# Reordering the opening stage of a transformer step: the order in which tokens, modulation weights and first products are taken

## The chip, the cores and the metric

The kernel runs on one core of a Trainium2 chip. The metric is the device time of one execution, in microseconds (us). The engines are TensorE (PE; its weight loads are PEld), VectorE (DVE), ScalarE (ACT), GpSimd (POOL) and SyncE (SP, which here only issues DMAs). Each engine works through its own list of instructions in the order in which the program wrote them, and waits where an operand of the next one isn't there yet.

## The reference, cut to what matters

One layer of a diffusion backbone runs over 1152 tokens (1024 latent ones, 128 context ones) of width 1024, in float32. The part that the change touches is the way from the tokens to the first columns of the input projection:

```python
mod = (silu(cond) @ w_mod + b_mod)[:, None, :]
sh1, sc1, g1, sh2, sc2, g2 = split(mod, 6)
h = rmsnorm(x, g_pre_mix) * (1.0 + sc1) + sh1
proj = h @ w_in        # q, k, v, xr, gr, xf
```

Behind it stand attention, a linear recurrence, a Fourier mixing, the output projection and a SwiGLU network, which are the other 95% of the time.

## The kernel before

Tokens lie in nine tiles of 128, three to a **chunk** of 384 columns (n = 0, 1, 2; the third chunk holds 256 latent and 128 context tokens). The width of 1024 is cut into eight slices (k = 0 to 7). Every product in full float32 precision is three matmuls in the fp32r type (mm3, L184 to L186): high part of the weights by low part of the data, high by high, low by high. So each operand is first split into a high part (a copy into fp32r) and a low part (the operand less its high part).

The opening stage makes h, transposed, and the first two of fourteen **units** (128 columns each) of the input projection. Its order is a table of short words, START, that a loop walks through; each word records its instructions at the end of the lists of their engines. Numbers behind a letter are its arguments:

- X t: load tile t of the tokens (SP). Q t: its squares summed on ACT, then the root of the mean on POOL (L178, L180). N t: the tile is scaled by it on DVE (L303).
- T n k0 k1 u m: PE turns slices k0 to k1 - 1 of chunk n (L313), in both tables always one slice, which is three transposes, into the bank psu[u][m]. C n k0 k1 e: the bank is copied to SBUF (xT), on DVE with e = 0, on ACT with e = 1.
- M s q: load a quarter of the modulation weights of step s (512 KB, six buffers). A s: 64 small matmuls that make shift and scale of slices 2s and 2s+1 (L345), and a copy (rows). B s: one transpose (L353) and four small DVE operations that leave them in M and S1 (L358, L359).
- L i: load the weights of unit i (two buffers). W i: their high part, on ACT. V i: their low part, on DVE.
- m n k: shift and scale of chunk n, slice k, twice: on ACT straight into the high part hh (L330), on DVE into u (L331). r n k e: the low part hl = u less hh, on DVE with e = 0, on POOL with e = 1 (L174).
- s n k: PE adds slice k of chunk n to units 0 and 1, six matmuls of 384 columns. The sums stand in psu[0][n] and psu[1][n], two of the same six banks that the transposes use, for all eight slices. One such word is called a **step** below; there are 24.
- D: PE multiplies zeros, before the first tokens are there. E: a small load that is used after the stage.

SP issues the loads in the order of X, M, L and E; a load into a buffer that is still read waits, and all loads behind it. Four large buffers hold the three chunks of tokens and then, in turn, the turned chunks xT. When the table is done, the six banks are copied out and the loop over units 2 to 13 (from L804 on) keeps PE at work.

Of the kernel before, what the change touches and what calls it, by code (L numbers as in the profile page):

```python
# [9 lines left out]
F32 = mybir.dt.float32  # L10
# [6 lines left out]
P = 128  # L17
D = 1024
# [6 lines left out]
NCH = T // CW  # L25
# [110 lines left out]


START = """
D9 D7 X0 Q0 X1 Q1 X2 X3 N0 X4 N1 Q2 X5 Q3 N2 Q4 T07802 X6 N4 T04510 T05611 T06712 X7 L0 C0781
C0451 C0561 C0671 Q5 T03402 T00110 T01211 T02312 N3 Q6 C0340 Q7 X8 C0010 C0120 C0230 N5 T11200  # L140
T12301 M00 N7 C1121 C1231 N6 T15611 T16712 T10110 T13400 T14501 Q8 C1341 C1451 W0 C1560 C1670
T17812 N8 M01 M02 M03 T25601 T26702 V0 C1011 T20110 T21211 A0 C2011 C2121 L1 M10 C2561 C2671
T23401 W1 C1780 M11 B0 M12 m10 r101 V1 C2341 T24502 T27812 m11 T22300 C2451 m00 C2231 r110 s10
C2781 r000 m21 M13 m20 r200 s11 m01 r010 M20 s00 A1 s20 M21 r210 B1 m02 M22 s01 M23 m03 r021 m22
s21 m23 M30 M31 r221 A2 r230 M32 m12 s02 m13 r120 L2 r130 s22 s23 M33 E B2 m14 s12 m05 r031 m04 r050
r141 r041 s13 s03 m24 L3 A3 m25 r250 s14 m15 B3 r150 m16 r241 r160 m26 s04 s24 m06 r061 m17 W2
r261 r170 m27 s05 m07 W3 s25 r271 V2 s15 s16 r071 s17 s06 V3 s26 L4 s07 L5 s27
"""

_OUTS = {"y": (T, D), "new_k": (P, 512), "new_v": (P, 512), "new_h": (2, 256)}  # L150
# [2 lines left out]
def _body(tc, nc, A):  # L153
    PE, ACT, DVE, POOL, SP = nc.tensor, nc.scalar, nc.vector, nc.gpsimd, nc.sync

    def pool(name, bufs=1, side="left", space=None, **kw):
        if space is not None:
            kw["space"] = space
        return tc.alloc_tile_pool(name=name, bufs=bufs, side=side, **kw)
# [34 lines left out]
    X1 = tc.dram_tile([T, D], F32, name="X1")  # L194
# [21 lines left out]
    st = pool("startup")  # L216
# [565 lines left out]
    f = P_["kq"] = pool("kq")  # L782
# [829 lines left out]
    for v, (g, cs) in enumerate(VIS):  # L1612
        last = v == NV_ - 1
        for c_ in ([(c,) for c in cs] if last else [cs]):
# [6 lines left out]
            for p in range(7):  # L1621
# [131 lines left out]
```

## Time and profile before

| | us |
|---|---|
| median of three runs | 1435.22 (1434.53, 1435.22, 1440.06) |
| the profiled execution | 1430.3, with a span of 1428.5 |
| PE busy | 1375.9 (96% of the span) |
| DVE, ACT, POOL busy | 822.0, 573.4, 427.6 |

The span is the time from the first to the last instruction in the trace; 1.8 us of the profiled execution lie around it. All times of rows below are from the start of the span. A busy PE is not a PE at its peak, since the ends of matmuls are modelled.

### The profile page before, as it was taken

To read this page: it belongs to the slowest core of one execution; us is meant where nothing else is said; L and a number is where in the kernel's file an instruction comes from. 1 tells how busy PE (TensorE), PEld (TensorE's weight loads), DVE (VectorE), ACT (ScalarE), POOL (GpSimd) and SP (SyncE) were. 2 spreads that over 40 slices of the span, in tenths; PEclk is the share of its full clock that TensorE was granted. 3 is DMA by queue.
4 is the path that set the end of the run, shared out by engine and by line. 5 is a ranking of instruction groups with operands and counts; after the bars stand their busy time and mean duration, and the time that the engine had idled before them with its cause. 6 is when DMAs were issued, how large, how long until landed. Compare 5 with 4: busy or idle time off the path is not lost.

```text
span 1428.5 us, 22758 instructions
## 1 busy us (share of the span) xinstructions
PE 1375.9 (96%) x8918; PEld 1248.9 (87%) x8918; DVE 822.0 (58%) x1247; ACT 573.4 (40%) x1138; POOL 427.6 (30%) x426
## 2 busy tenths in 40 slices
PE   7899999998999999998999999999999989999998
PEld 6887799888889888887899999999999968888886
DVE  5724464564888843667866767667666653243232
ACT  6511136734888863555322323223222342142120
POOL 2301111222666662447634334333423100000000
PEclk9999999999999999999999999999999999999999
DMA  8558840147755335563222312222222472334541
GB/s 328 178 202 276 266 158 31 63 158 174 179 136 146 96 108 166 176 209 111 78 93 64 101 59 93 84 74 99 67 77 82 137 275 89 115 109 166 182 151 59
DMA packets 108326, 193.40 MB, mean 135 GB/s; under 512 B 7701, under 2 KB 77754, under 8 KB 104762
## 3 DMA queue, kind: packets, MB, share of 16 engines
q1 hardware_dynamic: 108074, 191.41, 41.7%
q8 instruction: 71, 1.16, 0.4%
q10 hardware_dynamic: 144, 0.52, 0.1%
q14 instruction: 37, 0.30, 0.1%
HBM read 146.67 MB, written 45.24 MB: 134 GB/s over the span
## 4 chain that ended last, share of the span: by engine, by line
PE 49%; DVE 2%; issue 1%; ACT 1%; DMA 1%; POOL 0%; DVEq 0%; POOLq 0%; SPq 0%; ACTq 0%
PE g L186 10%; PE g L184 10%; PE g L185 10%; PE d L186 6%; PE d L184 6%; PE d L185 6%; DVE gu L174 1%; DMA hr<-HB 1%; DVE av L174 0%; ACT gu L168 0%; DMA raw_gu<-in_w_down 0%; DVE u L1530 0%; DVE hf L1530 0%; DVE hd L174 0%; ACT av L168 0%
## 5 line engine op out<-in xcount | busy, mean ns | idle before, releaser
L186 PE MATMUL g<-av,gu 128*128 128x320 f32 (+1 forms) x1232 | 364.2, 296 | 7.7 <-DVE gu L174 7.3
L184 PE MATMUL g<-av,gu 128*128 128x320 f32 (+1 forms) x1232 | 364.3, 296 | 1.2 <-ACT av L168 0.8
L185 PE MATMUL g<-av,gu 128*128 128x320 f32 (+1 forms) x1232 | 363.1, 295 | 0.0
L186 PEld LDWEIGHTS g<-av,gu 128*128 128x128 f32 x1232 | 232.1, 188 | 10.3 <-DVE gu L174 10.2
L184 PEld LDWEIGHTS g<-av,gu 128*128 128x128 f32 x1232 | 231.9, 188 | 2.3 <-issue 1.4
L185 PEld LDWEIGHTS g<-av,gu 128*128 128x128 f32 x1232 | 232.2, 188 | 0.0
L174 DVE TENSOR_TENSOR gu<-raw_gu,gu 128x512 fp32r<-128x512 f32 x139 | 141.2, 1023 | 40.1 <-ACT gu L168 40.1
L184 PE MATMUL pu<-hl,w 128*128 128x384 f32 x336 | 123.0, 366 | 4.6 <-POOL hl L174 3.8
L186 PE MATMUL pu<-hh,w 128*128 128x384 f32 x336 | 113.1, 337 | 0.0
L185 PE MATMUL pu<-hh,w 128*128 128x384 f32 x336 | 113.1, 337 | 0.0
L184 PE MATMUL d<-dw,hd 128*128 128x512 f32 x270 | 106.7, 395 | 3.2 <-DVE dw L174 3.1
L186 PE MATMUL d<-dw,hd 128*128 128x512 f32 x270 | 106.4, 394 | 0.9 <-DVE hd L174 0.9
L185 PE MATMUL d<-dw,hd 128*128 128x512 f32 x270 | 106.4, 394 | 0.0
L1371 POOL TENSOR_TENSOR raw_gu<-raw_gu,t 128x512 f32<-128x512 f32 x25 | 33.2, 1329 | 233.4 <-DVE gu L174 233.4
L1530 DVE TENSOR_TENSOR u<-g,u 128x320 f32<-128x320 f32 (+1 forms) x176 | 77.5, 450 | 29.8 <-PE g L186 29.8
L940 PE MATMUL s<-ks,qs 128*128 128x384 f32 x384 | 91.0, 358 | 3.0 <-ACT p L953 1.5
L946 DVE TENSOR_REDUCE nm<-s 128x1 f32<-128x1152 f32 x64 | 86.6, 1353 | 9.4 <-PE s L940 9.2
L953 ACT ACTIVATE p<-s,nm 128x1152 f32<-128x1152 f32 x64 | 78.2, 1222 | 29.5 <-DVE nm L946 16.4
L1672 ACT ACTIVATE t<-d 128x512 f32<-128x512 f32 x18 | 10.7, 596 | 186.4 <-PE d L186 186.4
L168 ACT ACTIVATE gu<-raw_gu 128x512 fp32r<-128x512 f32 x139 | 83.4, 620 | 3.5 <-DMA raw_gu<-in_w_down 3.4
L1080 POOL TENSOR_SCALAR fv<-fv 128x1 f32<-128x1 f32 x9 | 2.7, 303 | 271.5 <-ACT t L1672 271.5
L184 PEld LDWEIGHTS pu<-hl,w 128*128 128x128 f32 x336 | 63.3, 189 | 21.7 <-issue 14.1
(276 smaller groups left out, 2867.4 us busy)
## 6 DMA issues: line engine op xcount, KB each, us to landing
raw_gu<-in_w_gu SPq DMA_DIRECT2D x25, 1024.0 KB, 4.8
hr<-HB SPq DMA_DIRECT2D x32, 704.0 KB, 5.0
wmb<-in_w_mod SPq DMA_DIRECT2D x32, 512.0 KB, 5.0
raw_gu<-in_w_down SPq DMA_DIRECT2D x22, 512.0 KB, 4.2
HB<-hf SPq DMA_DIRECT2D x18, 576.0 KB, 3.1
x<-in_x SPq DMA_DIRECT2D x18, 512.0 KB, 4.6
wm<-in_w_mod SPq DMA_DIRECT2D x16, 512.0 KB, 7.7
raw<-in_w_in_u SPq DMA_DIRECT2D x14, 512.0 KB, 7.7
```

The source lines that it names most:

```text
L168: ACT.activation(out, in_, AF.Copy)
L174: eng.tensor_tensor(out, x, hi.bitcast(F32), op=OP.subtract)
L184: PE.matmul(out, wh, xl, start=first, stop=False)
L185: PE.matmul(out, wh, xh, start=False, stop=False)
L186: PE.matmul(out, wl, xh, start=False, stop=last)
L940: PE.matmul(b[:, j, :CW], q[:, st_, m, i * P:(i + 1) * P], ks[:, m, j * CW:(j + 1) * CW], start=(st_ == 0), stop=(st_ == 1))
L946: DVE.tensor_reduce(nm, s, axis=AX.XY, op=OP.max, negate=True)
L953: ACT.activation(p.rearrange("p (n c) -> p n c", c=CW), s, AF.Exp, bias=nm, accum_out=ss)
L1080: POOL.tensor_scalar(v[:, 0:1], v[:, 0:1], v[:, 1:2], D * EPS, op0=OP.add, op1=OP.add)
L1371: POOL.tensor_tensor(b21, b21, t2, op=OP.subtract)
L1530: add = lambda out, x: DVE.tensor_tensor(out, b, x, op=OP.add)
L1672: ACT.activation(t2, b, AF.Square, accum_out=fv[:, t, n:n + 1])
```

## The change

The table START is replaced, and nothing else of weight is: the three token buffers are now named before the loop and not at the first load of each chunk (they come in the same order as before). The words are the same ones but for three things: every low part r has e = 0, so none is left on POOL (eleven of 24 were there); of the 24 copies C, twelve are on DVE (seven were), and T takes the banks in another order; the order of the words is new throughout. As all lines behind the table move down by one, L184 to L186 are L185 to L187 in the changed kernel, L174 is L175 and so on.

```diff
 START = """
-D9 D7 X0 Q0 X1 Q1 X2 X3 N0 X4 N1 Q2 X5 Q3 N2 Q4 T07802 X6 N4 T04510 T05611 T06712 X7 L0 C0781
...
+D9 D7 X0 Q0 X1 Q1 X2 Q2 M00 M01 M02 M03 N0 N1 N2 X3 X4 X5 L0 L1 X6 X7 X8
...
-    raws, wsl, xts, xch, xT = {}, {}, {}, {}, {}
+    raws, wsl, xts, xT = {}, {}, {}, {}
+    xch = [st.tile([P, 3, D], F32, name=f"x{n}", tag="x", bufs=4) for n in range(NCH)]
 
     def load_x(t):
         n, i = divmod(t, 3)
-        if i == 0:
-            xch[n] = st.tile([P, 3, D], F32, name=f"x{n}", tag="x", bufs=4)
```

On SP the loads stood as nine token tiles, with unit 0's weights ahead of the ninth, then the sixteen quarters of modulation weights, with unit 1's weights behind the first four. Now they stand as three token tiles, four quarters, three token tiles, the weights of units 0 and 1, three token tiles, and twelve quarters; units 2 and 3 come behind all of these.

Three places show what that does to the lists. In the names, x0, x1, x2 are the chunks of tokens, xT0 to xT2 the same turned, pu with two digits is the bank psu[u][m], mod and rows belong to A, modt to B, w0 and w1 are the split weights of units 0 and 1, and ssx holds the sums of squares.

ScalarE, from the first squares on, in the kernel before:

```order
L299 ACTIVATE hh_88,ssx_115<-x0_142 128x1024 x3
L299 ACTIVATE hh_88,ssx_115<-x1_152 128x1024 x2
L168 ACTIVATE xT0_186<-pu02_119 128x384
L168 ACTIVATE xT0_186<-pu10_120 128x384
L168 ACTIVATE xT0_186<-pu11_121 128x384
L168 ACTIVATE xT0_186<-pu12_122 128x384
L299 ACTIVATE hh_88,ssx_115<-x1_152 128x1024
L299 ACTIVATE hh_88,ssx_115<-x2_171 128x1024 x2
L168 ACTIVATE xT1_228<-pu00_117 128x384
L168 ACTIVATE xT1_228<-pu01_118 128x384
L299 ACTIVATE hh_88,ssx_115<-x2_171 128x1024
```

and in the changed one, from the squares of chunk 1 on:

```order
L299 ACTIVATE hh_88,ssx_118<-x1_109 128x1024 x3
L330 ACTIVATE hh_88<-xT0_196,M_80,S1_81 128x384 x2
L169 ACTIVATE w0_280<-raw0_171 128x1024
L169 ACTIVATE w1_283<-raw1_173 128x1024
L169 ACTIVATE xT1_298<-pu12_125 128x384
L169 ACTIVATE xT1_298<-pu11_124 128x384
L169 ACTIVATE xT1_298<-pu12_125 128x384
L330 ACTIVATE hh_88<-xT1_298,M_80,S1_81 128x384 x2
L169 ACTIVATE xT1_298<-pu11_124 128x384
L299 ACTIVATE hh_88,ssx_118<-x2_110 128x1024 x3
L169 ACTIVATE xT2_373<-pu12_125 128x384 x2
```

The squares of chunk 2 stood behind the copies of chunk 0, the last of them behind two copies of chunk 1; now they stand behind the last copy of chunk 1, and behind four of the modulated slices (hh) and both weight splits.

VectorE, from the last norm of chunk 1 on, in the kernel before:

```order
L303 TENSOR_SCALAR x1_152<-x1_152,rsx_116 128x1024
L303 TENSOR_SCALAR x2_171<-x2_171,rsx_116 128x1024 x2
L170 COPY xT1_228<-pu11_121 128x384
L170 COPY xT1_228<-pu12_122 128x384
L303 TENSOR_SCALAR x2_171<-x2_171,rsx_116 128x1024
L174 TENSOR_TENSOR w0_252<-raw0_184,w0_252 128x1024
L170 COPY rows00_313<-mod00_280 128x128
L170 COPY xT1_228<-pu12_122 128x384
L358 TENSOR_TENSOR M_80<-modt00_332,vec_77 128x2x2
L359 SCALAR_TENSOR_TENSOR S1_81<-M_80,vec_77 128x2
L358 TENSOR_TENSOR M_80<-modt00_332,vec_77 128x2x2
```

and in the changed one, from the end of B0 on:

```order
L359 SCALAR_TENSOR_TENSOR S1_81<-M_80,vec_77 128x2
L303 TENSOR_SCALAR x1_109<-x1_109,rsx_119 128x1024
L331 TENSOR_SCALAR u0_0_271<-xT0_196,S1_81,M_80 128x384
L331 TENSOR_SCALAR u0_1_274<-xT0_196,S1_81,M_80 128x384
L175 TENSOR_TENSOR hl_89<-u0_0_271,hh_88 128x384
L175 TENSOR_TENSOR hl_89<-u0_1_274,hh_88 128x384
L303 TENSOR_SCALAR x1_109<-x1_109,rsx_119 128x1024
L175 TENSOR_TENSOR w0_280<-raw0_171,w0_280 128x1024
L175 TENSOR_TENSOR w1_283<-raw1_173,w1_283 128x1024
L171 COPY xT1_298<-pu02_122 128x384
L171 COPY xT1_298<-pu01_121 128x384
```

The norm of chunk 1's last tile (the last row on x1) was ahead of everything that belongs to the modulation; now the first modulation, two slices u and their low parts stand before it, and the copies out of the banks (xT1) stand behind the low parts of both weights.

TensorE, at the first steps, in the kernel before:

```order
L313 MATMUL pu11_121<-ident_78,x2_171 128x128 x3
L345 MATMUL mod00_280<-wm00_225,cm_93 32x128 x8
L345 MATMUL mod00_280<-wm01_260,cm_93 32x128 x8
L345 MATMUL mod00_280<-wm02_262,cm_93 32x128 x8
L345 MATMUL mod00_280<-wm03_264,cm_93 32x128 x8
L313 MATMUL pu01_118<-ident_78,x2_171 128x128 x3
L353 MATMUL modt00_332<-ident_78,rows00_313 128x128
L313 MATMUL pu02_119<-ident_78,x2_171 128x128 x3
L313 MATMUL pu12_122<-ident_78,x2_171 128x128 x3
L313 MATMUL pu00_117<-ident_78,x2_171 128x128 x3
L184 MATMUL pu01_118<-hl_89,w0_252 128x384
L185 MATMUL pu01_118<-hh_88,w0_252 128x384
```

and in the changed one, from the last matmul of the fourth step on:

```order
L187 MATMUL pu11_124<-hh_88,w1_283 128x384
L313 MATMUL pu02_122<-ident_78,x2_110 128x128 x3
L313 MATMUL pu12_125<-ident_78,x2_110 128x128 x3
L313 MATMUL pu02_122<-ident_78,x2_110 128x128 x3
L313 MATMUL pu12_125<-ident_78,x2_110 128x128 x3
L345 MATMUL mod01_384<-wm10_218,cm_93 32x128 x8
L345 MATMUL mod01_384<-wm11_220,cm_93 32x128 x8
L345 MATMUL mod01_384<-wm12_263,cm_93 32x128 x8
L345 MATMUL mod01_384<-wm13_265,cm_93 32x128 x8
L353 MATMUL modt01_423<-ident_78,rows01_417 128x128
L313 MATMUL pu02_122<-ident_78,x2_110 128x128 x3
L313 MATMUL pu12_125<-ident_78,x2_110 128x128 x3
```

Before, all 72 transposes and A0 stood ahead of the first step. Now 48 of them and A0 do, and the 24 of chunk 2 (x2) come in two groups of twelve behind the fourth step, with A1 and B1 between the groups.

## Rows read from the trace of the kernel before

**Rows 1.** The page, busy time and share of the span of each engine.

```profile
PE 1375.9 (96%) x8918; PEld 1248.9 (87%) x8918; DVE 822.0 (58%) x1247; ACT 573.4 (40%) x1138; POOL 427.6 (30%) x426
```

**Rows 2.** Timeline of TensorE: start, duration, operation, [idle before, releaser].

```profile
1.04 7.01 PE L374 MATMUL warm<-zero 128*128 128x128 f32 x32 [1.04 <-DVE zero L282]
...
11.23 4.20 PE L313 MATMUL pu<-ident,x 128*128 128x128 f32 x24 [1.14 <-DVE x L303]
17.01 2.29 PE L313 MATMUL pu<-ident,x 128*128 128x128 f32 x19 [1.57 <-DVE x L303]
...
22.89 1.96 PE L345 MATMUL mod<-wm,cm 128*32 128x128 f32 x64
...
28.68 0.44 PE L184 MATMUL pu<-hl,w 128*128 128x384 f32 x1 [2.09 <-POOL hl L174]
...
40.08 0.65 PE L345 MATMUL mod<-wm,cm 128*32 128x128 f32 x16 [1.17 <-DMA wm<-in_w_mod]
...
53.01 0.33 PE L184 MATMUL pu<-hl,w 128*128 128x384 f32 x1
...
54.05 0.33 PE L184 MATMUL pu<-hl,w 128*128 128x384 f32 x1
...
61.68 0.45 PE L184 MATMUL pu<-hl,w 128*128 128x384 f32 x1 [1.74 <-POOL hl L174]
...
64.80 0.41 PE L184 MATMUL pu<-hl,w 128*128 128x384 f32 x1 [0.74 <-DVE xft L170]
```

**Rows 3.** Single microseconds: busy of PE, PEld, DVE, ACT, POOL; granted clock; DMA share, GB/s.

```profile
11.00:12.00 1.00, 0.77 (x4) 0.77 (x5) 0.18 (x1) 1.00 (x3) 0.83 (x3) 0.50 1.05 430
...
27.00:28.00 1.00, 0.00 (x0) 0.00 (x0) 1.00 (x2) 1.00 (x3) 1.00 (x1) 1.00 1.00 385
```

**Rows 4.** Timeline of SyncE: the first loads, and four in a row.

```profile
1.64 4.08 SPq L233 DMA_DIRECT2D x<-in_x  x8
...
8.01 4.18 SPq L290 DMA_DIRECT2D wm<-in_w_mod  x4
```

**Rows 5.** Timeline of ScalarE.

```profile
5.37 1.06 ACT L299 ACTIVATE hh<-x 128x1024 fp32r<-128x1024 f32 x1 [1.23 <-DMA x<-in_x]
...
16.40 1.06 ACT L299 ACTIVATE hh<-x 128x1024 fp32r<-128x1024 f32 x1
17.37 0.19 ACT L299 ACTIVATION_READ_ACCUMULATOR hh<-x 128x1 f32 x1
...
24.16 1.08 ACT L168 ACTIVATE w<-raw 128x1024 fp32r<-128x1024 f32 x1
...
27.06 0.69 ACT L330 ACTIVATE hh<-xT,M,S 128x384 fp32r<-128x384 f32 x1
```

**Rows 6.** Timeline of VectorE.

```profile
18.58 1.42 DVE L303 TENSOR_SCALAR x<-x,rsx 128x1024 f32<-128x1024 f32 x2 [1.63 <-POOL rsx L180]
...
24.91 0.29 DVE L170 COPY rows<-mod 128x128 f32<-128x128 f32 x1 [2.19 <-PE mod L345]
25.11 0.55 DVE L170 COPY xT<-pu 128x384 f32<-128x384 f32 x1
...
26.08 0.16 DVE L359 SCALAR_TENSOR_TENSOR S<-M,vec 128x2 f32<-128x2 f32 x1
26.16 0.47 DVE L331 TENSOR_SCALAR u<-xT,S,M 128x384 f32<-128x384 f32 x1
26.56 1.21 DVE L174 TENSOR_TENSOR w<-raw,w 128x1024 fp32r<-128x1024 f32 x1
27.69 1.55 DVE L331 TENSOR_SCALAR u<-xT,S,M 128x384 f32<-128x384 f32 x2
29.16 1.02 DVE L174 TENSOR_TENSOR hl<-u,hh 128x384 fp32r<-128x384 f32 x2
30.09 1.24 DVE L331 TENSOR_SCALAR u<-xT,S,M 128x256 f32<-128x256 f32 x4
```

**Rows 7.** Timeline of GpSimd, the first low part.

```profile
26.86 1.77 POOL L174 TENSOR_TENSOR hl<-u,hh 128x384 fp32r<-128x384 f32 x1 [6.18 <-ACT hh L330]
```

More of the change, by code (lines that the diff above doesn't have):

```diff
@@ L138 @@
 START = """
-D9 D7 X0 Q0 X1 Q1 X2 X3 N0 X4 N1 Q2 X5 Q3 N2 Q4 T07802 X6 N4 T04510 T05611 T06712 X7 L0 C0781
[L140 to L147, printed above, removed]
+D9 D7 X0 Q0 X1 Q1 X2 Q2 M00 M01 M02 M03 N0 N1 N2 X3 X4 X5 L0 L1 X6 X7 X8
+T00101 T01211 T02302 T03412 T04500 T05610 C0010 C0121 C0230 C0341 T06701 T07811 C0450 C0561 C0670
+C0781 Q3 Q4 N3 M10 M11 A0 B0 M12 M13 N4 Q5 m00 m01 r000 r010 N5 W0 V0 W1 V1
+T10102 T11212 T12301 T13411 C1010 C1121 C1230 C1341 T14502 T15612 T16701 T17811 s00 s01 C1450 C1561
+m10 m11 r100 r110 C1670 C1781 Q6 Q7 Q8 N6 N7 s10 s11 N8
+M20 M21 T20102 T21212 C2010 C2121 T22302 T23412 C2230 C2341 A1 M22 M23 B1 m20 m21 r200 r210
+T24502 T25612 C2450 C2561 m02 m03 r020 r030 T26702 T27812 C2670 C2781 s20 s21 s02 s03 m12 m13 r120
+r130 M30 M31 s12 s13 m22 m23 r220 r230 A2 M32 M33 E L2 B2 L3 s22 s23 m04 m05 r040 r050 s04 s05 m14
+m15 r140 r150 s14 s15 m24 m25 r240 r250 A3 B3 s24 s25 m06 m07 r060 r070 W2 V2 s06 s07 m16 m17 r160
+r170 s16 s17 L4 m26 m27 r260 r270 W3 V3 s26 s27 L5
 """
```

## The prediction

> **What bounds the kernel now.** The page comes first: TensorE is busy for 96% of the span [rows 1], so what counts is where it has no work, and the change touches only the opening. There its timeline tells three stretches [rows 2]. Until 28.68 us TensorE does little but turn tokens: 24 transposes from 11.23 on, the next 19 from 17.01 on, both released by a norm on VectorE, and A0 at 22.89. From 28.68 on it runs the 24 steps, nearly without a break: six matmuls take 1.04 us (53.01 to 54.05), and it waits three times by over a microsecond, 2.09 and 1.74 us for low parts of GpSimd and 1.17 us for a load. At 64.80 unit 2 begins, 0.74 us behind the last step, which so ended at 64.06. From there on TensorE is full and every load is issued behind the opening, so I carry a shift of that end to the end of the kernel one for one.
>
> **The prices.** A square with the read of its sum takes 1.16 us on ScalarE (16.40 to 17.56), a weight's high part 1.08, a modulated slice 0.69 [rows 5]. From the end of a square to its norm on VectorE, by way of GpSimd, 1.02 us pass (17.56 to 18.58); a norm takes 0.71 in a row of two, a copy 0.55, a weight's low part 1.21, u 0.47, a low part 0.51 in a row of two, the u of two slices of chunk 2 1.24; from the rows copy of a step A to the last small operation of its B 1.33 us (24.91 to 26.24) [rows 6]. A takes 1.96 and 24 transposes take 4.20 at a mixed clock, 0.175 each, or 0.12 (2.29 by 19) at the full one [rows 2]. Loads of 512 KB come every 1.28 us (four issues in 4.18, the last one's own time of about 0.33 taken off), and the first, issued at 1.64, lands just ahead of 5.37 [rows 4, 5].
>
> **Loads.** M03 is now the seventh and lands at 13.0 (5.3 + 6 x 1.28), the weights of unit 1 the twelfth, 19.4, the last tokens the fifteenth, 23.3, M13 the nineteenth, 28.4. All of these come ahead of the work below, so none sets a time. The new order of the token buffers costs nothing either: the same four buffers are taken in the same turn.
>
> **The walk through the changed opening.** I follow the lists and put the row's price on each entry.
>
> 1. Chunk 0 is turned as before, to 15.43 (11.23 + 4.20). A0 then ends at 17.4 and not at 24.85: a gain of 7.5 us on the first modulation.
> 2. The squares of chunk 1 stand behind the copies of chunk 0 on ScalarE: from 15.9 (15.4 and a copy of about 0.5) the first ends at 17.1, the third at 19.4. The first norm of chunk 1 starts at 18.1 (17.1 + 1.02) and ends at 18.8; VectorE then does A0's rows and B0, to 20.2, the second norm, to 20.9, two u, to 21.8, two low parts, to 22.8, and only then the third norm, though that was ready at 20.4. By the sum it ends at 23.6; neighbours overlap by some 0.08 us (26.16 + 0.47 against 26.56) [rows 6], so I take 23.3. Before, that norm let TensorE go at 17.01.
> 3. Chunk 1's transposes: the first twelve last from 23.3 to 25.4. The other twelve need banks back: two of the six hold the sums of chunk 0 from now on, and the copies that free the rest stand behind both weights' low parts on VectorE: 23.3 + 2 x 1.21 + 0.55 = 26.3. ScalarE splits the high parts from 21.6 (20.2 + 2 x 0.69) to 23.8, in time. Then 2.1 us more: the first step starts at **28.4**, where it was 28.68. The seven microseconds of step 1 are gone, and 24 transposes of chunk 2 are still to come, which before were done.
> 4. Four steps, 4.2 us, to 32.6. Their later low parts are ready by 29.4 (26.3, two copies, two u, two low parts) and hold nothing up.
> 5. The squares of chunk 2 are behind chunk 1's last copy on ScalarE: from 28.9, three to 32.4; the last norm from 33.4 to 34.1, whatever time the tokens landed. TensorE waits for it, turns twelve, to 36.2, and does A1, to 38.2.
> 6. VectorE goes through A1's rows and B1, to 39.5, the u and low parts of chunk 2's first two slices (1.24 + 1.02), to 41.8, and a copy that frees a bank for the last six transposes, to 42.3; then two u and two low parts of chunk 0, 1.96, and the copy that frees the bank of chunk 2's sums, to 44.8. TensorE has twelve transposes to do in all this. The fifth step starts at **44.9**.
> 7. Twenty steps take 20.8 us, A2 and A3 3.9, and in each of their B the rows copy holds TensorE for about 0.4. At the end unit 2's low part V2 stands ahead of the last u: from B3 on, two modulated slices, W2, V2, two u and a low part are 1.38 + 1.08 + 1.21 + 0.94 + 0.51 = 5.1 us, in which TensorE has some 3.9 us of work, a wait of 1.2. Together 26.7, to 71.6.
>
> **TensorE's clock.** From 8.05 (1.04 + 7.01) to 11.23 TensorE had almost nothing to do, and at 11 to 12 us the granted clock was 0.50, 1.2 GHz; a gap of 2.09 us before 28.68 left it at 1.00, 2.4 GHz [rows 2, 3]. The changed opening has gaps far longer than the first: 17.4 to 23.3, and 38.2 to 44.9 but for twelve transposes. I charge the transposes at the mixed price (done above) and the fifth and sixth step at half clock, up to 2 x 1.04; taking 1.7 of it, the stage ends at 73.3. The Trainium skill, "TensorE: Matmul & The Clock Gate", section "HAM oscillation", holds that work in short bursts between waits finds the clock throttled anew in each burst. By that rule the sum is the 73.3 above; with none of it, rival B's.
>
> **What is moved and costs nothing.** Eleven low parts go from GpSimd to VectorE, 5.6 us (11 x 0.51), and five copies from ScalarE, 2.8. From 44.9 on VectorE has 16 blocks of u and low part at about 1.0, twice 1.33, and two low parts of weights, 2.4: some 21 us under TensorE's 26.7, so it is no new bound; if TensorE's waits were gone, it would be close to one. On SP, M22 to M31 wait for A1 and land long ahead of A2 at about 53. Units 2 and 3 are now queued behind M32 and M33, which wait for A2 (about 55): the fifth of these lands by 64 (55 + 3.7 + 4 x 1.28, the 3.7 from the first load), W2 comes at about 66. That cover is 2 us thin (rival C).
>
> **Sum.** 73.3 less 64.06: the opening ends 9.2 us later. On the profiled execution, 1430.3 us (span 1428.5 and 1.8 around it), that gives 1439.5; the median of the runs shown stands 4.9 us above that execution, and the forecast is made against the median: 1435.2 + 9.2 = **1444.4**. Half a percent, 7.2 us, is about what a measurement of this kernel tells from no change.
>
> **Rivals.** *A, faster: GpSimd's waits were the price.* Both waits on low parts of GpSimd, 3.8 us (2.09 + 1.74) [rows 2], cannot come back, and a u beside a low part on GpSimd takes 1.1 us where 0.47 is usual (27.69, 1.55 for two, while GpSimd works from 26.86 to 28.63) [rows 6, 7]. If the rest only changes places, 1435.2 - 3.8 = 1431.4. It decides when the 24 steps, three A and 24 transposes (25.0 + 5.9 + 2.9, about 1 for B) run without a wait from a first step before 29.3 (64.06 - 34.8). Against it: steps 5 and 6 put waits of 1.5 and over 4 us right there. The Trainium skill, "SBUF - State Buffer", section "Who interferes with whom", has GpSimd and VectorE share one pair of ports that only one can hold; by that rule this relief is sure, and the trace agrees on the pair above. *B, the clock stays full.* Transposes at 0.12 bring the fifth step to 43.6, and without the 1.7 the end is 70.3: 6.2 us late, 1441.4, within the half percent. For it: the clock stayed up over 2.09 us. Against: it fell at 11. *C, late loads.* A2's last quarter came 1.17 us late before [rows 2]. If the loads behind A2 come at half their rate, W2 and V2 hold the last four steps for about 4 us: 1448.4. *D, the shift is taken back later,* since some later wait is not for TensorE: 1435 to 1440. Against it, nothing behind the opening is issued earlier than its end allows.
>
> **How the numbers follow.** Forecast (7.2 to 12 us late) 0.65, C 0.10, B 0.17, D 0.03, A 0.05. Slower by over 0.5%: 0.65 + 0.10 = 0.75; the same: 0.17 + 0.03 = 0.20; faster: 0.05. The range goes from 1437 (B with two or three of the short waits of step 7 and of VectorE's queue less) to 1450 (C with the clock low once more); A, half of D and what lies beyond C stay out, under 0.2.
>
> **What would show it.** In the changed trace: A0 from about 15.4; the first step near 28.4, the fifth near 45; TensorE idle between, released by norms and copies of VectorE; a granted clock of 0.50 in the twenties and again in the forties; GpSimd without low parts; unit 2 near 74. A first step before 26, or a fifth before 40, would prove me wrong.

## The result and the profile after

The changed kernel takes 1443.11 us (median of seven runs, 1441.23 to 1448.36) where the kernel before takes 1435.22 (median of seven, 1428.71 to 1440.06): 7.9 us more, a ratio of 1.006 with a 95% interval of 1.0032 to 1.0088. That is slower by a little over half a percent; the lower end of the interval lies inside the half percent. The forecast was 1444.4 us, 9.2 us more. The profiled execution took 1442.63 us, with a span of 1440.8.

On the page the busy line answers [rows 1]. GpSimd has 15 us less to do, and TensorE is busy for 10 us more with the same number of matmuls:

```profile
PE 1385.9 (96%) x8918; PEld 1258.4 (87%) x8918; DVE 825.6 (57%) x1263; ACT 572.4 (40%) x1133; POOL 412.5 (29%) x415
```

TensorE's timeline of the opening, as in [rows 2] (start, duration, operation, idle time before and what ended it):

```profile
11.58 4.95 PE L313 MATMUL pu<-ident,x 128*128 128x128 f32 x22 [1.03 <-DVE x L303]
16.46 2.21 PE L345 MATMUL mod<-wm,cm 128*32 128x128 f32 x64
20.04 0.33 PE L353 MATMUL modt<-ident,rows 128*128 128x128 f32 x1 [1.38 <-DVE rows L171]
...
24.17 2.39 PE L313 MATMUL pu<-ident,x 128*128 128x128 f32 x10 [2.05 <-DVE x L303]
26.91 2.82 PE L313 MATMUL pu<-ident,x 128*128 128x128 f32 x12 [0.34 <-DVE xT L171]
29.38 0.67 PE L185 MATMUL pu<-hl,w 128*128 128x384 f32 x1
...
36.27 0.66 PE L313 MATMUL pu<-ident,x 128*128 128x128 f32 x4 [1.14 <-DVE x L303]
...
38.52 3.10 PE L345 MATMUL mod<-wm,cm 128*32 128x128 f32 x64
...
45.67 0.87 PE L313 MATMUL pu<-ident,x 128*128 128x128 f32 x6 [2.64 <-DVE xT L171]
47.85 0.69 PE L185 MATMUL pu<-hl,w 128*128 128x384 f32 x1 [1.31 <-DVE xT L171]
...
49.94 0.52 PE L185 MATMUL pu<-hl,w 128*128 128x384 f32 x1
...
72.81 0.44 PE L185 MATMUL pu<-hl,w 128*128 128x384 f32 x1 [0.93 <-DVE hl L175]
...
78.04 0.41 PE L185 MATMUL pu<-hl,w 128*128 128x384 f32 x1 [0.74 <-DVE xft L171]
```

A0 is done 6 us earlier than before, yet the first step begins at 29.38, the fifth at 47.85, and the opening ends at 77.30 (78.04 less the wait of 0.74) where it ended at 64.06. Every wait in it is released by VectorE: a norm (x), a copy that frees a bank (xT), the rows of a step A, a low part (hl). None is released by GpSimd or by a load.

ScalarE's and VectorE's timelines show why the norms of chunk 2 are late. The squares begin behind the last copy of chunk 1, at 30.44; a norm follows its square by way of GpSimd, and the last one ends at 36.21:

```profile
30.07 0.47 ACT L169 ACTIVATE xT<-pu 128x384 f32<-128x384 f32 x1
30.44 1.05 ACT L299 ACTIVATE hh<-x 128x1024 fp32r<-128x1024 f32 x1
```

```profile
24.03 2.35 DVE L175 TENSOR_TENSOR w<-raw,w 128x1024 fp32r<-128x1024 f32 x2
26.30 1.01 DVE L171 COPY xT<-pu 128x384 f32<-128x384 f32 x2
...
35.46 0.75 DVE L303 TENSOR_SCALAR x<-x,rsx 128x1024 f32<-128x1024 f32 x1 [0.71 <-POOL rsx L181]
...
44.12 1.03 DVE L175 TENSOR_TENSOR hl<-u,hh 128x384 fp32r<-128x384 f32 x2
45.06 0.55 DVE L171 COPY xT<-pu 128x384 f32<-128x384 f32 x1
45.53 0.86 DVE L331 TENSOR_SCALAR u<-xT,S,M 128x384 f32<-128x384 f32 x2
46.30 1.02 DVE L175 TENSOR_TENSOR hl<-u,hh 128x384 fp32r<-128x384 f32 x2
47.24 0.55 DVE L171 COPY xT<-pu 128x384 f32<-128x384 f32 x1
```

The copies at 26.30 stand behind both weights' low parts, the ones at 45.06 and 47.24 behind u and low parts, just as the lists have them. Each frees a bank for which TensorE waits.

Four stretches of five microseconds (busy time of PE, PEld, DVE, ACT, POOL; granted clock of TensorE; DMA share; GB/s), as in [rows 3]:

```profile
10.00:15.00 5.00, 3.85 (x17) 3.56 (x18) 2.27 (x5) 0.98 (x2) 0.65 (x2) 0.52 1.03 417
...
25.00:30.00 5.00, 4.66 (x22) 4.26 (x21) 4.05 (x8) 2.50 (x5) 0.00 (x0) 0.50 1.03 419
...
35.00:40.00 5.00, 3.54 (x39) 2.71 (x42) 1.87 (x3) 1.86 (x5) 0.43 (x1) 0.75 0.00 2
...
45.00:50.00 5.00, 3.02 (x13) 2.79 (x14) 5.00 (x14) 3.42 (x7) 0.00 (x0) 0.78 0.64 198
```

The clock is low early, at 25 to 30, in part at 35 to 40 and again when the fifth step begins. A1 takes 3.10 us instead of 1.96, and the fifth step 2.09 (47.85 to 49.94) instead of 1.04.

### The profile page after: what moved, and what is told of

It is laid out like the page before. It is cut to its first block, busy times and chain, and to the rows that moved or that the text cites. A ratio compares the mean times of both kernels' runs of the same rounds, so it can differ in the third digit from the quotient of the medians.

```text
span 1440.8 us, 22755 instructions
## 1 busy us (share of the span) xinstructions
PE 1385.9 (96%) x8918; PEld 1258.4 (87%) x8918; DVE 825.6 (57%) x1263; ACT 572.4 (40%) x1133; POOL 412.5 (29%) x415
## 4 chain that ended last, share of the span: by engine, by line
PE 49%; DVE 2%; DMA 1%; issue 1%; ACT 1%; POOL 0%; DVEq 0%; SPq 0%; POOLq 0%; ACTq 0%
PE g L187 10%; PE g L185 10%; PE g L186 10%; PE d L187 6%; PE d L185 6%; PE d L186 6%; DVE gu L175 1%; DMA hr<-HB 1%; DMA raw_gu<-in_w_down 0%; DVE av L175 0%; DVE u L1530 0%; ACT hd L169 0%; ACT gu L169 0%; DVE hd L175 0%; ACT av L169 0%
## 5 line engine op out<-in xcount | busy, mean ns | idle before, releaser
L187 PE MATMUL g<-av,gu 128*128 128x320 f32 (+1 forms) x1232 | 365.7, 297 | 6.0 <-DVE gu L175 5.9
L185 PE MATMUL g<-av,gu 128*128 128x320 f32 (+1 forms) x1232 | 366.2, 297 | 1.3 <-DVE u L1530 1.2
L186 PE MATMUL g<-av,gu 128*128 128x320 f32 (+1 forms) x1232 | 365.1, 296 | 0.0
L187 PEld LDWEIGHTS g<-av,gu 128*128 128x128 f32 x1232 | 233.9, 190 | 7.5 <-DVE gu L175 7.3
L185 PEld LDWEIGHTS g<-av,gu 128*128 128x128 f32 x1232 | 233.7, 190 | 1.9 <-ACT s L169 1.4
L186 PEld LDWEIGHTS g<-av,gu 128*128 128x128 f32 x1232 | 234.0, 190 | 0.0
L175 DVE TENSOR_TENSOR gu<-raw_gu,gu 128x512 fp32r<-128x512 f32 x139 | 141.5, 1025 | 40.1 <-ACT gu L169 40.1
L185 PE MATMUL pu<-hl,w 128*128 128x384 f32 x336 | 123.3, 367 | 3.0 <-DVE xT L171 1.3
L187 PE MATMUL pu<-hh,w 128*128 128x384 f32 x336 | 113.7, 338 | 0.0
L186 PE MATMUL pu<-hh,w 128*128 128x384 f32 x336 | 113.5, 338 | 0.0
L185 PE MATMUL d<-dw,hd 128*128 128x512 f32 x270 | 106.9, 396 | 2.6 <-DVE dw L175 2.5
L187 PE MATMUL d<-dw,hd 128*128 128x512 f32 x270 | 106.5, 394 | 0.9 <-DVE hd L175 0.9
L186 PE MATMUL d<-dw,hd 128*128 128x512 f32 x270 | 106.4, 394 | 0.0
L1672 ACT ACTIVATE t<-d 128x512 f32<-128x512 f32 x18 | 10.7, 596 | 182.8 <-PE d L187 182.8
L185 PEld LDWEIGHTS pu<-hl,w 128*128 128x128 f32 x336 | 64.0, 190 | 19.5 <-issue 13.2
```

Source lines behind the costliest of these rows:

```text
L175: eng.tensor_tensor(out, x, hi.bitcast(F32), op=OP.subtract)
L185: PE.matmul(out, wh, xl, start=first, stop=False)
L186: PE.matmul(out, wh, xh, start=False, stop=False)
L187: PE.matmul(out, wl, xh, start=False, stop=last)
L1672: ACT.activation(t2, b, AF.Square, accum_out=fv[:, t, n:n + 1])
```

## The experiments

The theory, called "lists" below: TensorE waits because squares, norms and bank-freeing copies stand late in the lists of ScalarE and VectorE, and the low clock adds to it. Its rivals: VectorE is overloaded by the eleven low parts that came from GpSimd; the load order costs; the half clock is the main loss; TensorE's idle time is free room. In the experiments that leave the table one line shorter, L185 to L187 are L184 to L186, and so on.

All profiles in one table. "First" and "fifth" are the starts of the first and fifth step in the table's order, "end" the end of the last step, "behind" the time from unit 2's first matmul to TensorE's last one:

| kernel | first | fifth | end | behind | ratio of times to before (95%) |
|---|---|---|---|---|---|
| before | 28.68 | 35.11 | 64.06 | 1357.3 | 1 |
| before, profiled again | 28.85 | 35.29 | 68.69 | 1356.7 | |
| changed | 29.38 | 47.85 | 77.30 | 1356.4 | 1.006 (1.0032 to 1.0088) |
| changed, profiled again | 28.90 | 47.26 | 76.52 | 1356.9 | |
| changed, low parts on GpSimd | 26.83 | 43.28 | 74.82 | 1359.8 | 1.0062 (1.0042 to 1.0081) |
| before, low parts on VectorE | 27.99 | 35.64 | 67.78 | 1358.2 | 0.999 (0.997 to 1.001) |
| before, changed load order | 35.25 | 41.70 | 73.91 | 1359.7 | 1.0054 (1.0033 to 1.0075) |
| changed, norms earlier | 27.45 | 45.76 | 75.73 | 1357.4 | 1.0059 (1.0036 to 1.0081) |
| changed, zeros | 26.57 | 44.35 | 72.25 | 1358.0 | 1.0026 (1.0011 to 1.0040) |
| changed, gap filled | 29.22 | 38.79 | 73.40 | 1362.3 | 1.0041 (1.0022 to 1.0059) |
| before, zeros | 30.42 | 36.80 | 66.05 | 1358.8 | 1.0001 (0.9982 to 1.0020) |
| changed, norms and zeros | 27.80 | 45.95 | 73.85 | 1356.3 | 1.0039 (1.0021 to 1.0056) |
| before, free buffer | 27.31 | 36.47 | 62.49 | 1357.5 | 0.9947 (0.9927 to 0.9966) |
| the same, zeros | 27.82 | 35.42 | 61.47 | 1357.9 | 0.9937 (0.9916 to 0.9958) |

### Both kernels once more

No edit; a second profile of each.

> The kernel before, unchanged, profiled once more, to tell how much of a profiled opening is chance. Theory 'lists': the first step within 2 us of 28.68, the wait of A2 for its last quarter somewhere between 1 and 3 us, the opening's end at 64 to 67 us, and the time behind it within 3.5 us of 1357, as in the runs so far. Rival (the first profile of before was typical): all within 0.3 us of the first.

> The changed kernel, unchanged, profiled once more, for the same reason as the kernel before. Theory 'lists': its releasers are those of the first profile, and the opening ends between 72 us (with the clock full) and 78 us. Rival (the first profile was an unlucky one): 72 to 73.5 us.

The kernel before ended its opening at 68.69 this time, beyond the 67 expected, the changed one at 76.52, inside its bounds. The two profiles of before thus differ by 4.6 us; the second execution took 1434.36 us, near the median of 1435.22, the first 1430.3, so the second is the more usual one. The first steps agree, within 0.2 us; the difference comes at A2. Its last quarter of weights:

```profile
41.97 1.08 PE L345 MATMUL mod<-wm,cm 128*32 128x128 f32 x16 [2.87 <-DMA wm<-in_w_mod]
```

It waits 2.87 us, not the 1.17 of [rows 2], and then works at half clock (16 records in 1.08 us, there 0.65). In five profiles with the old lists (these two and three variants below) the wait was 1.17, 2.87, 3.02, 3.08 and 0.71 us: long in three of five. The difference of the two openings is 13.2 us by the first profiles, 7.8 by the second, 10.5 by their means; the timed runs differ by 7.9.

### The low parts on GpSimd, undone

The eleven words of the table that differ, in its order (r names a low part, its last digit the engine, 1 for GpSimd):

```diff
-r100 r020 r220 r030 r140 r040 r240 r060 r260 r270 r070
+r101 r021 r221 r031 r141 r041 r241 r061 r261 r271 r071
```

> The changed kernel with one part undone: the eleven low parts that GpSimd had before are on GpSimd again, all else as changed. Theory 'lists' (the opening is late because squares, norms and the copies that free banks stand late in the lists of ScalarE and VectorE, so that TensorE waits for them): the three late places stay, the fifth step begins within 1.5 us of 47.85 and the opening ends at 77 to 80 us, since GpSimd's low parts are slower (1.77 against 0.51 us) and lengthen the VectorE work beside them. Rival 'VectorE overloaded' (the eleven low parts moved to VectorE are what TensorE waits behind): 5.6 us of VectorE work go, and the opening ends at 71 to 73 us.

The time is that of the changed kernel, 1.0062 against 1.006, so the eleven low parts on VectorE are not what costs in sum. The opening's end, 74.82, is between the two forecasts, and the fifth step's 43.28 is no hit for "lists" either. Most of this is the clock: A1 took 1.95 us here and not 3.10, the 22 transposes of chunk 0 2.62 and not 4.95, and A1 ends 3.7 us earlier (37.9 against 41.6):

```profile
11.04 2.62 PE L312 MATMUL pu<-ident,x 128*128 128x128 f32 x22 [1.14 <-DVE x L302]
...
42.04 0.88 PE L312 MATMUL pu<-ident,x 128*128 128x128 f32 x6 [2.76 <-DVE xT L170]
```

The long wait for the copy stays (2.76 us, 2.64 in the changed kernel). From the end of A1 to the fifth step pass 5.4 us instead of 6.2: the low parts of chunk 0's slices 2 and 3 no longer stand ahead of a copy on VectorE, and the fifth step waits 0.37 us instead of 1.31. So the rival "VectorE overloaded" holds at that one place, for 0.8 us, which are lost again behind the fifth step (31.5 us to the end instead of 29.45, three waits for GpSimd of 1.25 us among them). By the stretch up to A1, a single profile of such an opening can move by some 3 us with the clock.

### All low parts on VectorE in the kernel before

The same eleven words, the other way:

```diff
-r101 r021 r221 r031 r141 r041 r241 r061 r261 r271 r071
+r100 r020 r220 r030 r140 r040 r240 r060 r260 r270 r070
```

> The kernel before with one part of the change alone: all low parts on VectorE, the order of the table as before. The GpSimd relief as the prediction's rival A has it: both waits on low parts (2.09 and 1.74 us) go, the opening ends at 60.3 us instead of 64.06 and the kernel takes 3.8 us less, ratio 0.997. Theory 'lists', in which VectorE's queue takes part of this back because copies and norms now stand behind 5.6 us more work: 61.5 to 63.5 us, 0.5 to 2.5 us less. Rival 'VectorE overloaded': the opening ends later than 64.06, at 65 to 68 us.

The time is unchanged: 0.999, 0.997 to 1.001, and the opening ends at 67.78, against 64.06 and 68.69. That end misses the bounds of "lists" and lies in those of "VectorE overloaded" (65 to 68). But what is late is A2, by a wait of 3.02 us for a load and a low clock behind it, and the second profile of before, with the low parts on GpSimd, has the same and ends 0.9 us later still. GpSimd's two waits of 3.8 us go, and three waits for low parts of VectorE come, 3.2 us together:

```profile
27.99 0.41 PE L184 MATMUL pu<-hl,w 128*128 128x384 f32 x1 [0.93 <-DVE hl L174]
30.28 0.45 PE L184 MATMUL pu<-hl,w 128*128 128x384 f32 x1 [0.80 <-DVE hl L174]
42.47 1.08 PE L345 MATMUL mod<-wm,cm 128*32 128x128 f32 x16 [3.02 <-DMA wm<-in_w_mod]
57.11 0.44 PE L184 MATMUL pu<-hl,w 128*128 128x384 f32 x1 [1.48 <-DVE hl L174]
```

So the prediction's rival A falls: the relief of 3.8 us is worth 0.6 (3.8 less 3.2), because the moved low parts queue behind others on VectorE.

### The changed load order in the kernel before

The loads alone, in their order; X are tokens, M quarters of modulation weights, L a unit's weights:

```diff
-X0 X1 X2 X3 X4 X5 X6 X7 L0 X8 M00 M01 M02 M03 L1 M10 M11 ...
+X0 X1 X2 M00 M01 M02 M03 X3 X4 X5 L0 L1 X6 X7 X8 M10 M11 ...
```

> The kernel before with the changed order of loads alone: three token tiles, four quarters of modulation weights, three token tiles, both units' weights, three token tiles, twelve quarters; all compute in the order of before. Theory 'lists': in the changed kernel no load was waited for, but in the old lists chunk 2 is turned ahead of the first step and its tokens now land at 22 to 25 us and not at about 13, so the first step moves from 28.68 to 33 to 36 us and the opening ends at 68 to 73 us. Rival 'loads cost nothing': chunk 2's squares and norms find room anyway, first step within 1.5 us of 28.68 and the end at 63 to 66 us.

The first step comes at 35.25, the end at 73.91, just beyond the upper bound; the kernel loses as much as by the whole change. In the old lists the squares of chunk 1 stand ahead of the copies of chunk 0, and wait for tokens that now land later; TensorE then waits 4.04 us for such a copy. ScalarE, and TensorE behind it:

```profile
15.05 1.06 ACT L299 ACTIVATE hh<-x 128x1024 fp32r<-128x1024 f32 x1 [5.61 <-DMA x<-in_x]
```

```profile
17.92 3.25 PE L313 MATMUL pu<-ident,x 128*128 128x128 f32 x14 [4.04 <-ACT xT L168]
```

Part of the 6.6 us at the first step is the clock: it was low from 10 to 27 us, and 19 transposes of chunk 0 took 4.32 us where [rows 2] have 2.29. The load order is not free in itself: with the old lists it costs. In the changed kernel, whose lists ask for chunks 1 and 2 late, no wait of TensorE is released by a load, so what costs there is the lists. The changed lists with the old load order were not run; whether they would lose less is open.

### The norms of chunk 2 earlier

```diff
-W1 V1 T10102 ... s00 s01 C1450 ... C1781 Q6 Q7 Q8 N6 N7 s10 s11 N8
+W1 V1 Q6 Q7 Q8 T10102 ... s00 s01 N6 N7 N8 C1450 ... C1781 s10 s11
```

> The changed kernel with one thing moved: the three squares of chunk 2 stand ahead of the first transposes of chunk 1, and so ahead of the copies of chunk 1 on ScalarE, and its three norms ahead of VectorE's copies of slices 4 to 7 of chunk 1. Theory 'lists': TensorE's wait for the last norm of chunk 2 (1.14 us, and the idle time around it) goes, chunk 2 is turned right behind the fourth step, the fifth step begins 2 to 3 us earlier (45 to 46 us) and the opening ends at 73 to 75 us instead of 77.30. Rival 'half clock' (what costs is the low TensorE clock after each gap): the gap only changes its place, end within 1 us of 77.3. Rival 'VectorE overloaded': the three norms delay the first step by as much as they gain, end within 1 us of 77.3 too, but with the clock full where the gap was.

The fifth step comes at 45.76 as "lists" has it, 1.5 to 2.1 us earlier than in the two profiles of the changed kernel, but the end, 75.73, by only 0.8 to 1.6, outside the 73 to 75 of "lists" and not within the 1 us of 77.3 that the rivals allowed. The time does not move (1.0059). TensorE's wait for the last norm is gone, and a new one of 2.18 us stands ahead of the third step:

```profile
32.00 0.44 PE L184 MATMUL pu<-hl,w 128*128 128x384 f32 x1 [2.18 <-DVE xT L170]
...
43.58 1.54 PE L312 MATMUL pu<-ident,x 128*128 128x128 f32 x6 [2.65 <-DVE xT L170]
```

The three norms now stand ahead of the copies of chunk 1: what was moved up pushed something else that TensorE waits for.

### Zeros in the idle stretches of the changed kernel

```diff
-A0 B0 ... s11 ... A1 M22 M23 B1 ... T25612 ... T27812
+A0 D6 B0 D9 D3 ... s11 D7 ... A1 D2 M22 M23 B1 ... T25612 D9 D3 ... T27812 D6
```

> The changed kernel with matmuls of zeros added on TensorE in its idle stretches of the opening (6 behind A0, 12 behind B0, 7 behind the fourth step, 2 behind A1, 12 and 6 among the last transposes of chunk 2), 45 in all, so that TensorE is hardly idle while it waits; lists of the other engines unchanged. Theory 'lists': the granted clock stays at 1.00 through the opening, which gives back what the half clock took (20 us of the profiled opening ran at 0.50, some of it idle or not TensorE's to decide), 2.5 to 5 us; the releasers stay (norms and copies of VectorE), the fifth step begins at 43 to 45.5 us and the opening ends at 72 to 75 us, still 8 to 11 us behind the kernel before. Rival 'half clock' (the low clock is most of the loss): the end comes to within 3 us of 64.06. Rival 'zeros in the way': the clock stays up but the added matmuls delay what they stand before, end at 77 us or later.

The granted clock is 1.00 in the whole opening, which ends at 72.25, inside the bounds of "lists". In the timed runs the zeros give back 4.9 us (0.34% of 1435: from 1.0060 to 1.0026). The intervals overlap (1.0032 to 1.0088, 1.0011 to 1.0040). By the traces an opening at the full clock is 4.3 to 5.1 us shorter (76.52 or 77.30 less 72.25), so the low clock cost some 4 to 5 us. The releasers of the real work stay:

```profile
10.00:15.00 5.00, 3.86 (x63) 3.50 (x67) 2.98 (x5) 1.96 (x4) 0.53 (x1) 1.00 1.02 411
...
11.38 2.62 PE L312 MATMUL pu<-ident,x 128*128 128x128 f32 x22 [1.14 <-DVE x L302]
...
25.28 1.53 PE L312 MATMUL pu<-ident,x 128*128 128x128 f32 x12 [1.38 <-DVE xT L170]
...
33.98 0.66 PE L312 MATMUL pu<-ident,x 128*128 128x128 f32 x4 [0.83 <-DVE x L302]
...
44.35 0.42 PE L184 MATMUL pu<-hl,w 128*128 128x384 f32 x1
```

From the end of the fourth step (30.16 + 1.04 = 31.2) to the fifth pass 13.2 us, in the changed kernel 13.4 (34.4 to 47.85): this stretch is set by the lists and not by the clock. What the full clock gives stands ahead of the first step, 2.8 us, and behind the fifth, 1.5.

Not all of this is the zeros' doing. The 2.8 us are there by the end of A0 (the transposes and A0 took 4.5 us instead of 7.1, and from A0's end to the first step 10.7 us pass in both), and ahead of A0 stand no zeros that the changed kernel lacks: there TensorE has the same instructions in both. The clock was full there by chance; in the run with earlier norms and zeros (below), also without more zeros ahead of A0, the same transposes took 4.12 us. To the zeros themselves this trace leaves some 2.2 us.

### The same in the kernel before

```diff
-D9 D7 X0 ... T11200 ... T17812 ... s10 ... s07
+D9 D7 D9 X0 ... D9 T11200 ... D9 D2 T17812 ... D9 D5 s10 ... D9 D2 s07
```

> The kernel before with matmuls of zeros in its idle stretches of the opening, as the changed kernel had them: 9 more ahead of the first tokens, 9 and 11 where it waits for a norm and a copy of chunk 1, 14 ahead of the first step, 11 ahead of the last but one; the idle time inside A2, behind a load, can't be filled. It separates the order of the lists from the clock. Theory 'lists': at a full clock the order alone costs what the two kernels with zeros differ by: this one ends its opening at 62 to 65 us against 72.25 of the changed one with zeros, 7 to 10 us. Rival 'half clock' (the orders are equal once the clock is): this one ends within 3 us of 72.25, so not before 69. Rival 'zeros gain as much here': the opening comes to 59 to 61 us, and the difference to the changed kernel stays 11 us or more.

The end is 66.05, past the 65 that "lists" allowed and short of the 69 of its rival; the time is that of before, 1.0001. The zeros were in the way at three places. The last transposes of chunk 1 and the first of chunk 2, 15 in a row, begin at 21.78 behind zeros, though VectorE's copies for which they wait in the first profile of before were done at 20.14; the first step comes at 30.42, though its low part was done at 29.27; and the last but one at 63.70, though its low part was done at 62.87:

```profile
19.00 2.94 PE L374 MATMUL warm<-zero 128*128 128x128 f32 x22
21.78 1.80 PE L313 MATMUL pu<-ident,x 128*128 128x128 f32 x15
...
27.05 3.61 PE L374 MATMUL warm<-zero 128*128 128x128 f32 x28
30.42 0.42 PE L184 MATMUL pu<-hl,w 128*128 128x384 f32 x1
```

With the clock at 1.00 in both, the changed lists end 6.2 us later (72.25 less 66.05), less than the 7 to 10 expected and by no means equal. The three delays are up to 1.6, 1.1 and 0.8 us; without them, and with the same clock, the difference would be up to 9.7 us, an estimate. In the timed runs 0.25% are left, 3.6 us, with intervals that overlap.

### The longest gap filled

A1, B1 and four steps stand ahead of chunk 2's transposes:

```diff
-s11 N8 M20 M21 T20102 T21212 C2010 ...
+s11 N8 A1 M20 M21 M22 M23 B1 m02 m03 r020 r030 s02 s03 m12 m13 r120 r130 s12 s13 T20102 T21212 C2010 ...
```

> The changed kernel with work moved into its longest idle stretch: A1, B1 and the four steps of slices 2 and 3 of chunks 0 and 1 stand right behind the fourth step, ahead of all transposes of chunk 2, which now follow them. Theory 'lists': TensorE has 6 us of work while chunk 2's squares and norms run, but the transposes, copies, u and low parts of chunk 2 come as much later, and VectorE's and ScalarE's lists hold the same work: the end moves by less than 2 us from where it is, 75 to 78 us. Rival 'idle time' (what is lost is just TensorE's idle time between the fourth and the fifth step, and any work put there gains it): the 2.64 and 1.14 us waits go, and the end comes to 71 to 73 us.

The end, 73.40, lies between the two forecasts, and the time, 1.0041, between before and changed, with an interval that overlaps those of the changed kernel and of the one with zeros. It is faster in the trace by 3 to 4 us, and most of that can be the clock: A1 took 1.95 us instead of 3.10, and the fifth and sixth step 1.07 us each, together 1.6 us less than in the changed kernel, some 2.8 us in sum (an estimate from these rows). The time behind the opening is 1362.3 us in this profile, 2.5 to 6 us more than in the others, so its whole execution does not follow its opening. The wait for the copy stays, 2.19 us, and one of 1.97 us for a low part is new:

```profile
38.79 0.45 PE L184 MATMUL pu<-hl,w 128*128 128x384 f32 x1 [1.97 <-DVE hl L174]
...
48.47 0.88 PE L312 MATMUL pu<-ident,x 128*128 128x128 f32 x6 [2.19 <-DVE xT L170]
```

### Earlier norms and zeros together

The two edits of the changed kernel in one, with 48 zeros, placed where its waits are (ahead of the third step, among them).

> The changed kernel with chunk 2's squares and norms ahead of chunk 1's last copies (as in the run with the norms moved) and with zeros in the idle stretches. In the run with the norms moved alone, TensorE's wait for the last norm of chunk 2 went, but a wait of 2.18 us for VectorE's copies came ahead of the third step. Theory 'lists': the moved norms stand ahead of copies that TensorE needs as well, so the wait only changes its owner; with the clock full the fifth step begins within 1.5 us of 44.35 (43 to 45.8) and the opening ends at 71 to 74 us. Rival 'one misplaced entry' (the late norms of chunk 2 are the fault of the order): the fifth step begins before 42 us and the opening ends before 70.

The fifth step comes at 45.95, 0.15 us beyond the bound of "lists" and 4 us from the rival's, the end at 73.85: in this trace moving the norms gains nothing over the zeros alone. The clock was not out of the way everywhere. It was low from 11 to 14.5 us, and the zeros ahead of the third step let it begin at 33.35, 1.0 us behind the copy that it needs:

```profile
11.34 4.12 PE L312 MATMUL pu<-ident,x 128*128 128x128 f32 x22 [1.14 <-DVE x L302]
...
29.98 3.61 PE L373 MATMUL warm<-zero 128*128 128x128 f32 x28
```

Without these two, about 1.2 and 1.0 us, the fifth step would begin at about 43.7 and the opening end at about 71.6 us (an estimate): still little gained over the zeros alone, and beyond the 42 and 70 of the rival. So chunk 2's norms are not one misplaced entry whose move would mend the order; that no other order of these lists would do better is not shown.

Timed in the same rounds, this kernel and the one before with zeros differ by 4.7 us (1439.98 and 1435.33), and their intervals, 1.0021 to 1.0056 and 0.9982 to 1.0020, are apart: with zeros in both, the changed order still costs time.

### A version that beats both

It is the kernel before with two of the eleven low parts on VectorE, the ones TensorE waited for, and with three quarters of modulation weights in the buffer that the tokens of chunk 2 leave:

```diff
-r101 ... r071
+r100 ... r070
-        t = wm[s, q] = st.tile([P, 2, 2, 256], F32, name=f"wm{s}{q}", tag="wm", bufs=6)
+        i = 4 * s + q - 10
+        if 0 <= i < 3:
+            if i == 0:
+                wmx.append(st.tile([P, 3, D], F32, name="wmx", tag="x", bufs=4))
+            t = wm[s, q] = wmx[0][:, i].rearrange("p (k g c) -> p k g c", k=2, g=2)
+        else:
+            t = wm[s, q] = st.tile([P, 2, 2, 256], F32, name=f"wm{s}{q}", tag="wm", bufs=6)
```

(M21, M22, M23 and M30 move up in the table, to M20.)

> A version meant to beat both: the kernel before with (1) two of its eleven GpSimd low parts on VectorE, those that TensorE waited for (chunk 1 slice 0, 2.09 us, and chunk 0 slice 7, 1.74 us), and (2) three quarters of modulation weights (the last two of step 2 and the first of step 3) loaded into the buffer that chunk 2's tokens leave free, so that they need not wait for A1. Theory 'lists': the wait for the last quarter of A2 (1.17 us in the profile of before, 3.0 in two of its variants) goes, the GpSimd waits shrink to about 1 and 0.5 us, the opening ends at 60 to 62.5 us and the kernel takes 2 to 5 us less than before, ratio 0.9965 to 0.9985. Rival 'low clock and VectorE take it back': end within 1 us of 64.06, ratio 1.000.

It takes 1428.98 us against 1435.93 of before in the same rounds: 0.9947, 0.9927 to 0.9966, 7 us less and more than was expected. The opening ends at 62.49, and of the low parts TensorE waits for VectorE's for 0.93 and 0.81 us and for GpSimd's for 0.22. A2 runs without a wait, one half from the old buffers (wm) and one from the new (wmx), and the clock stays up behind it, where the second profile of before had 0.63 and 0.69. A2, then 40 to 50 us of this kernel, then the same of before:

```profile
38.73 1.08 PE L351 MATMUL mod<-wm,cm 128*32 128x128 f32 x32
39.63 1.06 PE L351 MATMUL mod<-wmx,cm 128*32 128x128 f32 x32
```

```profile
40.00:45.00 5.00, 5.00 (x53) 4.76 (x42) 4.46 (x12) 1.83 (x4) 1.60 (x2) 1.00 0.62 229
45.00:50.00 5.00, 5.00 (x83) 4.55 (x82) 4.21 (x9) 3.83 (x8) 3.30 (x3) 1.00 0.00 0
```

```profile
40.00:45.00 5.00, 3.03 (x22) 2.62 (x23) 1.88 (x5) 0.23 (x1) 0.40 (x1) 0.63 0.98 329
45.00:50.00 5.00, 5.00 (x22) 4.97 (x22) 1.68 (x8) 0.76 (x2) 0.00 (x0) 0.69 0.63 249
```

The gain beyond the expected 5 us would fit a wait of 3 us at A2 and a stretch at half clock behind it, as in three of the five profiles with the old lists; that is argued, not shown. The opening ends 1.6 and 6.2 us earlier than in the two profiles of before. How the gain divides between the load and the two low parts was not run.

Zeros in its idle stretches (9 more at the start, 6, 7, 6 and 5 at its four waits):

> The version with two low parts moved and three quarters loaded into the free token buffer, with matmuls of zeros in its idle stretches: 9 more ahead of the first tokens, 6 and 7 at the waits for chunk 1, 6 and 5 ahead of the first two steps. Its profiled opening had about 10 us at half clock, in which 24 transposes took 5.38 us instead of 2.6 and steps were slower. Theory 'lists plus clock': the transposes give little, since norms release what follows, and the steps and A1 1 to 2 us: the opening ends at 60 to 61.5 us instead of 62.49, the time is 1 to 2 us less, ratio to before 0.993 to 0.9945. Rival 'zeros in the way': end at 62.5 to 64 us, ratio 0.995 to 0.997.

The opening ends at 61.47 and the ratio is 0.9937 (0.9916 to 0.9958), both inside the bounds of "lists plus clock" (its 61.5 only just). The nine zeros at the start did not hold the clock: it was 0.50 from 12 to 15 us, and the 22 transposes of chunk 0 took 4.29 us. The two versions can't be told apart by their times.

## Why the prediction was right, and where it was not

**The direction and its cause were right.** The third norm of chunk 1 behind the first modulation (step 2), the copies behind both weights' low parts (step 3), the squares of chunk 2 behind chunk 1's last copy (step 5), the copies behind u and low parts (step 6): each stands in the trace as the releaser that was named. Only one of them, chunk 2's norms, was moved by an experiment, and another wait took its place. That the order costs time apart from the clock is shown with the clock at 1.00 in both openings (72.25 against 66.05) and by the two kernels with zeros that were timed side by side; how much each single place costs rests on the traces. The waits of 0.4 at each B and of 1.2 at V2 (step 7) came out at 0.41 and 0.93. The loads set no time, as said; rival C's late loads did not occur. Rival D falls too: the time behind the opening is 1356.4 and 1356.9 us in the changed kernel, 1357.3 and 1356.7 in the kernel before.

**The end was worked out 4 us too early:** 73.3, measured 77.30 and 76.52. The 4.0 us of the first profile by steps: A0 ends at 18.7 and not 17.4, and the first step begins at 29.38 instead of 28.4, 1.0 us; the four steps take 5.0 instead of 4.2, 0.8, with the clock at 0.50 in the first of them; from there to the fifth 13.4 instead of 12.3, 1.1; and from the fifth to the end 29.45 instead of 28.4, 1.05. Two terms were mis-sized. One is the clock: I took 1.7 us and a mixed price for the transposes, worth 3.0 together by the distance to rival B; the opening at full clock shows 4.3 to 5.1. I had looked for the low clock in the twenties and forties and found it there, but not for A1 at 3.10 us nor a second low stretch under chunk 0's transposes, which took 4.95 us for 22. The other is the price of a step: from the fifth on, with the clock full (44.35 to 72.25), 27.9 us pass where steps, A, B and V2 summed to 26.7. A step costs 1.04 in a row, as [rows 2] show, but 1.13 to 1.17 behind an A or a B or ahead of one.

**The total came out near by luck: the baseline missed by about as much as the end, and the two cancel.** The 9.2 us were 73.3 less 64.06; the opening of before ended at 64.06 and 68.69 in its two profiles. Had both ends been taken as their means, 66.4 and 76.9, the sum would be 10.5; the timed runs say 7.9 by the medians and 8.6 by the ratio. One profile of before carried a term, A2's wait, of which nothing told whether 1.17 us was usual. Setting the shift against the median of the runs, and not the profile's own 1430.3, was the right choice: that execution was on the short side of its kernel's runs.

**Rival A** was priced right as to the two waits and wrong as to what takes their place, which the prediction's own words against it ("steps 5 and 6 put waits of 1.5 and over 4 us right there") did not need to decide: even in the old order the relief is 0.6 us. The Trainium skill's page "SBUF - State Buffer", section "Who interferes with whom", has the two engines share a pair of ports. For a pair of u that agrees, 0.86 us for two in the changed kernel against 1.55 in [rows 6]; the time of the kernel did not follow.

**Rival B** came about in the profile with zeros: it said 70.3 for a full clock, and 72.25 was measured; of the 1.95 between them 1.2 is the price of the steps. The prediction had the low clock in the transposes and in the fifth and sixth step; it also fell on A1 and on the first of the four early steps. The Trainium skill, "TensorE: Matmul & The Clock Gate", section "HAM oscillation", has each burst between waits find the clock throttled anew. The trace agrees in part: 0.50 at 25 to 30 us and again as the fifth step begins, but 1.00 behind the gap of 2.09 us in [rows 2], and at the 22 transposes it differs from profile to profile.

## What to carry to other kernels

When an opening's order is changed, list for each wait of the engine that bounds it what stands ahead of its releaser on the other engines. Here an early first modulation was worth nothing, because the next norms, squares and bank-freeing copies went behind what it set free. Profile the kernel before twice if a term of the sum is a wait for a load, and price work behind a wait at both levels of the clock, as a range: here the same work behind the same wait ran at either. Where a load waits for a buffer, look for another buffer that is free by then; the version that did so, with two low parts moved as well, was the only one here, without zeros or with them, that beat the kernel before.

## What the runs showed of the hardware

- The low clock behind the same wait is partly chance. The 22 transposes of chunk 0 took 4.95 and 4.22 us in two profiles of the changed kernel and 2.62 in the one with its low parts on GpSimd, with the same instructions of TensorE ahead of them. The Trainium skill, "TensorE: Matmul & The Clock Gate", section "What's actually happening", calls the number of slow matmuls "run-variable"; these rows agree.
- The wait inside A2 was followed by a clock of 0.50 in all three profiles in which it was 2.87 to 3.08 us, and not in the two in which it was 1.17 and 0.71 (the last with zeros).
- With matmuls of zeros in its idle stretches, 45 in all, the changed kernel kept the clock at 1.00 from A0 to the end of its opening at 72 us; ahead of A0 that was chance. Zeros that are still running when the real work is ready delay it: by 1.1 us ahead of the first step of before, by up to 1.6 ahead of 15 of its transposes.
- Of two loads of 512 KB issued 0.4 us apart, behind a pause of the queue, the second landed 3.4 us (before), 4.7 us (its second profile), 5.0 us (all low parts on VectorE), 5.1 us (changed load order) and 2.8 us (zeros) behind the first, where loads in a row land 1.28 us apart.
